# A Mixer and Expert Block on One Core: 32 Early Expert Chunks Instead of 24, Low Parts on VectorE, Small Groups Normed with the Dense Frames

## The chip, the cores and the metric

The kernel runs on one core of one Trainium2 chip. TensorE multiplies matrices, VectorE (DVE) and ScalarE (ACT) work on tiles, GpSimd (POOL) does some tile work and issues the indirect gathers, SyncE (SP) issues transfers. The metric is the device time of one execution in microseconds.

## The reference, cut to what matters

512 frames of width 2048 go through one layer (an RWKV mixer and a sparse attention, gated and projected) and then a PEER feed-forward with 16384 experts and a final RMSNorm. The change touches the feed-forward and the norm:

```
def _peer_ffn(h, w_query, sub_keys, expert_u, expert_v):
    q = (h @ w_query).reshape(B, T, PEER_HEADS, 2, PEER_HALF)      # 8 heads, 2 halves of 128
    s = einsum('bthcq,hcnq->bthcn', q, sub_keys)                   # 128 sub-keys per half
    s1, i1 = top_k(s[..., 0, :], 16); s2, i2 = top_k(s[..., 1, :], 16)
    cand = s1[..., :, None] + s2[..., None, :]
    top_s, pos = top_k(cand, 16); eid = i1*128 + i2 at pos
    gate = softmax(top_s)
    act = gelu(einsum('nd,nhkd->nhk', hx, expert_u[eid]), exact)
    return einsum('nhk,nhkd->nd', gate * act, expert_v[eid])

h = h + _peer_ffn(rmsnorm(h), ...)
return rmsnorm(h)
```

## The kernel before, in words

All large products take a float32 weight tile of 128 x 1024 apart into a high part (ScalarE, line 204) and a low part (VectorE, line 206; in the head loop GpSimd, line 208) and run three matmuls per pair of factors: high by high, high by low, low by high. `load_w` loads the tile on SyncE's queue and raises the priority of its three instructions by 100, which puts them that much ahead in the order of their engines. Each engine runs its instructions in a fixed order. `pieces` hands out a product of 2048 rows in four pieces of 12 matmuls.

The first 1700 us (mixer, attention, projection) are not touched. Then:

*Head loop* (`route`, lines 1122 to 1175). For each of 8 heads and 2 halves: the sub-keys are loaded (line 1128), the query is computed (48 matmuls of 512 columns), then the scores, and on VectorE the 16 best by `top16`. From the two halves the 16 best pairs follow (lines 1141 to 1168). After each head four pieces of the early chunks and two items (below) are put in.

*Early chunks* (`early`, list EARLY). An expert chunk e is 128 experts; `act` multiplies its 2048 x 128 keys with the 336 dense frames and applies gelu. A group `cg` has 8 chunks, 16 groups in all. For 24 chunks this is done already in the route, and the activations are saved to memory (d_a): the first two of each even group, the first of each odd one.

*Gate phase* (lines 1201 to 1225). 84 turns of four frames each: ScalarE, GpSimd and VectorE make one-hot masks (`oa`, `ob`), TensorE multiplies them to gates (`pg`, eight instructions a turn), ScalarE copies them to Gs, and after every fourth turn they go to memory (d_g). 64 pieces of the early chunks are spread evenly over the 84 turns, and every sixth turn has one item.

*Pack* (lines 1006 to 1010). ScalarE and VectorE copy the frames of the dense part into ph and pl.

*Dense stage* (`experts`). 336 frames go through all experts. For each group the gates G are loaded (1253), the activations of the 8 chunks are computed (the early ones loaded from d_a, line 1271), multiplied with G and split (`gated`), and then for each of 16 blocks of 128 output columns 8 x 3 matmuls add up the values (1293 to 1295) and VectorE adds them to accT (1300). In the first group the early chunks stand last.

*Items* (`gathered`). The other 176 frames take their experts' rows one by one: GpSimd gathers 128 rows of 8 KB (line 1040, three buffers `rows`), VectorE multiplies and sums them (1050, `up`) or adds them to `out` (1062, `down`). They are three groups (GROUPS): 128 frames with all 128 rows, 32 frames in four parts, 16 frames in eight parts. The small groups are folded by TensorE (1074), added to the residual, normed and stored (1076 to 1083). `step` calls an item so often that all are through shortly before the end; an item's instructions stand behind the last low part.

*End* (`turned`, `final`). The dense result is transposed, the residual added, normed, and stored: two tiles of 128 frames and one of 80.

## Time and profile before

| | |
|---|---|
| median of 3 runs | 4027.23 us (4023.66 to 4030.58) |
| the profiled execution | 4027.87 us, span 4026.1 us |
| TensorE busy | 3873.1 us (96%), mean granted clock 0.987 |
| VectorE busy | 2851.7 us (71%) |
| ScalarE busy | 1399.9 us (35%) |
| GpSimd busy | 1076.6 us (27%) |
| transfers | 946.17 MB, mean 235 GB/s |

Busy times are sums over the whole span and say nothing of which engine limits a stage. Matmuls are pipelined and overlap in the records, so the pace of TensorE is read from how many start in a stretch. Lines as L1223 are lines of the kernel; `wk`, `mm` and `po` are the tiles in TensorE's accumulators (`po` belongs to the early chunks). A row of a timeline gives the start, the length, the engine (a q behind it: its queue), the line, the tiles and, in brackets, the engine's idle time before it and what ended that.

### The profile page before, as it was taken

How to read it: one execution, taken by the hardware profiler on the slowest of the kernel's cores; microseconds unless marked ns; L12 is line 12 of the kernel's file. 1: busy time of each engine (PE TensorE's matmuls, PEld its weight loads, DVE VectorE, ACT ScalarE, POOL GpSimd, SP SyncE). 2: the span in 40 equal slices, each digit the busy share in tenths (PEclk: the TensorE clock that was granted, in tenths of full speed). 3: DMA queues.
4: the chain of work that ended last, by engine and by line, in shares of the span. 5: the costliest groups of instructions: out<-in, count | busy, mean ns of one | idle time of the engine just before them, and what ended most of it. 6: DMA issues, size and time to landing. Idle time of an engine off the chain costs nothing.

```text
span 4026.1 us, 57532 instructions
## 1 busy us (share of the span) xinstructions
PE 3873.1 (96%) x22241; PEld 3505.8 (87%) x22241; DVE 2851.7 (71%) x4738; ACT 1399.9 (35%) x2048; POOL 1076.6 (27%) x1012
## 2 busy tenths in 40 slices
PE   7999999999999999999989799999999999999998
PEld 6787778888887788777879799999999999999998
DVE  5445589434444553379988689888788978998885
ACT  4222323222324422232278333333323333333333
POOL 2000211101004300064367233233233323333320
PEclk9999999999999999999999899999999999999999
DMA  4343852333226443374478799999999989999994
GB/s 149 119 134 123 196 181 81 96 107 95 90 83 211 140 138 139 105 260 162 169 220 269 277 350 371 369 369 366 323 342 366 371 302 358 372 366 367 368 346 153
DMA packets 258290, 946.17 MB, mean 235 GB/s; under 512 B 28224, under 2 KB 77504, under 8 KB 209280
## 3 DMA queue, kind: packets, MB, share of 16 engines
q1 hardware_dynamic: 132528, 445.76, 31.9%
q0 software_dynamic: 82144, 474.71, 31.8%
q10 hardware_dynamic: 43344, 22.02, 1.9%
q8 instruction: 175, 2.87, 0.3%
q14 instruction: 99, 0.81, 0.1%
HBM read 866.18 MB, written 76.12 MB: 234 GB/s over the span
## 4 chain that ended last, share of the span: by engine, by line
PE 39%; DMA 4%; DVE 3%; issue 2%; ACT 1%; POOL 1%; DVEq 0%; SPq 0%; ACTq 0%; POOLq 0%
PE wk L1293 7%; PE wk L1295 7%; PE wk L1294 7%; PE mm L224 5%; PE mm L225 5%; PE mm L223 5%; DMA rows<-in_rv_dram,eid 2%; PE wk L1223 1%; DMA rows<-in_ru_dram,eid 1%; POOL rows L1040 1%; DVE wlo L206 1%; DVE out L1062 1%; PE po L223 1%; PE po L224 1%; PE po L225 1%
## 5 line engine op out<-in xcount | busy, mean ns | idle before, releaser
L204 ACT ACTIVATE whi<-raw 128x1024 fp32r<-128x1024 f32 x758 | 803.2, 1061 | 1902.2 <-PE mm L224 1015.7
L206 DVE TENSOR_TENSOR wlo<-raw,whi 128x1024 fp32r<-128x1024 f32 x726 | 890.1, 1227 | 630.1 <-ACT whi L204 567.6
L1293 PE MATMUL wk<-Wh,whi 128*128 128x336 f32 x2048 | 653.9, 320 | 25.7 <-ACT Wh L236 25.7
L1294 PE MATMUL wk<-Wl,whi 128*128 128x336 f32 x2048 | 650.9, 318 | 4.7 <-DVE Wl L237 4.7
L1295 PE MATMUL wk<-Wh,wlo 128*128 128x336 f32 x2048 | 650.6, 318 | 0.2 <-DVE wlo L206 0.2
L223 PE MATMUL mm<-ph,whi 128*128 128x336 f32 x1664 | 526.7, 317 | 7.1 <-ACT ph L1009 7.1
L225 PE MATMUL mm<-ph,wlo 128*128 128x336 f32 x1664 | 527.3, 317 | 1.5 <-DVE wlo L206 1.5
L224 PE MATMUL mm<-pl,whi 128*128 128x336 f32 x1664 | 526.6, 316 | 0.0
L223 PE MATMUL mm<-xh,whi 128*128 128x512 f32 x1168 | 473.4, 406 | 2.8 <-ACT xh L355 1.5
L225 PE MATMUL mm<-xh,wlo 128*128 128x512 f32 x1168 | 468.5, 401 | 6.0 <-DVE wlo L206 6.0
L224 PE MATMUL mm<-xl,whi 128*128 128x512 f32 x1168 | 470.5, 403 | 0.6 <-POOL xl L357 0.5
L1040 POOL DMA_INDIRECT rows<-in_rv_dram,eid x176 | 284.0, 1613 | 593.0 <-DVE out L1062 494.7
L1062 DVE SCALAR_TENSOR_TENSOR out<-rows,act,out 128x2048 f32<-128x2048 f32 x173 | 406.0, 2347 | 41.6 <-DMA rows<-in_rv_dram,eid 40.8
L1040 POOL DMA_INDIRECT rows<-in_ru_dram,eid x176 | 273.2, 1552 | 602.9 <-DVE act L1050 486.4
L1050 DVE CUSTOM_DVE_ANT_0 rows<-rows,h2t 128x2048 f32<-128x2048 f32 x176 | 411.6, 2346 | 26.2 <-DMA rows<-in_ru_dram,eid 26.2
L1293 PEld LDWEIGHTS wk<-Wh,whi 128*128 128x128 f32 x2048 | 387.6, 190 | 29.4 <-ACT Wh L236 29.1
L1294 PEld LDWEIGHTS wk<-Wl,whi 128*128 128x128 f32 x2048 | 388.5, 190 | 6.7 <-DVE Wl L237 6.2
L1295 PEld LDWEIGHTS wk<-Wh,wlo 128*128 128x128 f32 x2048 | 388.6, 190 | 1.1 <-DVE wlo L206 0.7
L223 PEld LDWEIGHTS mm<-ph,whi 128*128 128x128 f32 x1664 | 313.3, 188 | 7.7 <-ACT ph L1009 7.3
L225 PEld LDWEIGHTS mm<-ph,wlo 128*128 128x128 f32 x1664 | 312.8, 188 | 1.9 <-DVE wlo L206 1.8
L224 PEld LDWEIGHTS mm<-pl,whi 128*128 128x128 f32 x1664 | 313.7, 189 | 0.5 <-issue 0.5
L225 PEld LDWEIGHTS mm<-xh,wlo 128*128 128x128 f32 x1168 | 221.8, 190 | 60.4 <-DVE wlo L206 6.9
(441 smaller groups left out, 6284.1 us busy)
## 6 DMA issues: line engine op xcount, KB each, us to landing
raw<-in_pu_dram SPq DMA_DIRECT2D x256, 512.0 KB
raw<-in_pv_dram SPq DMA_DIRECT2D x256, 512.0 KB
raw<-in_w_in_dram SPq DMA_DIRECT2D x146, 512.0 KB
d_g<-Gs ACTq DMA_DIRECT2D x21, 1024.0 KB
G<-d_g POOLq DMA_DIRECT2D x16, 1344.0 KB
raw<-in_wbr_dram SPq DMA_DIRECT2D x32, 512.0 KB
raw<-in_wout_dram SPq DMA_DIRECT2D x32, 512.0 KB
raw<-in_wpq_dram SPq DMA_DIRECT2D x32, 512.0 KB
```

Source lines behind the costliest of these rows:

```text
L204: nc.scalar.activation(hi, raw, AF.Copy)
L206: self.last = nc.vector.tensor_tensor(lo, raw, hi.bitcast(F32), op=ALU.subtract).ins
L223: nc.tensor.matmul(ps, hi[:, s], xh, start=k == 0, stop=False)
L224: nc.tensor.matmul(ps, hi[:, s], xl, start=False, stop=False)
L225: nc.tensor.matmul(ps, lo[:, s], xh, start=False, stop=k == nk - 1)
L1040: nc.gpsimd.indirect_dma_start(out=r, out_offset=None, in_=table, in_offset=bass.IndirectOffsetOnAxis(ap=eid[:, s:s + 1], axis=0))
L1050: v.tensor_tensor_reduce(r, r, h, 1.0, 0.0, op0=ALU.mult, op1=ALU.add, accum_out=self.act_[i][:, s:s + 1])
L1062: v.scalar_tensor_tensor(o, r, act[:, s:s + 1], o, op0=ALU.mult, op1=ALU.add)
L1223: mmul(pg[:, 128 * u:128 * u + 128], oa, ob, start=True, stop=True)
L1293: mmul(ps, hi[:, s], wh, start=j == 0, stop=False)
L1294: mmul(ps, hi[:, s], wl, start=False, stop=False)
L1295: mmul(ps, lo[:, s], wh, start=False, stop=j == 7)
```

## The change

EARLY has the first two chunks of every group, 32 in all. In the route 32 pieces lie in the head loop as before, 90 in the gate phase and 6 behind it. In the head loop the low parts of the query weights are made by VectorE as everywhere else, the sub-keys of all heads are loaded by one transfer ahead of it, and each head has one item instead of two; in the gate phase every seventh turn has an item instead of every sixth. In the first dense group the order of the chunks is 2 to 5, 0, 1, 6, 7, for the activations and for the value matmuls; the saved activations are loaded on ScalarE's queue. The two small groups no longer norm their frames: they store the sum with the residual to memory (d_s), it is loaded into the 48 free partitions of the last dense tile, and is normed and stored with it.

```diff
@@ -41,7 +41,7 @@
 
 GROUPS = ((160, 16, 8), (128, 32, 4), (0, 128, 1))
 
-EARLY = [8 * g + j for g in range(16) for j in range(2 - g % 2)]
+EARLY = [8 * g + j for g in range(16) for j in range(2)]
 
 VEC = {}
 _o = 0
@@ -169,7 +169,7 @@
     def __init__(self, tc, io, out, dbg=None):
         self.tc, self.nc, self.io, self.out, self.dbg = tc, tc.nc, io, out, dbg or {}
         self.fins = ExitStack()
-        self.wx, self.nw, self.low = None, 0, self.nc.vector
+        self.wx, self.nw = None, 0
         self.blocks = ((0, 128), (1, 128), (2, ND - 256))
 
     def pool(self, name, bufs=1, **kw):
@@ -202,10 +202,7 @@
             hi = ps.tile([128, 1024], F32R, tag="whi", name="whi")
             lo = ps.tile([128, 1024], F32R, tag="wlo", name="wlo")
             nc.scalar.activation(hi, raw, AF.Copy)
-            if self.low is nc.vector or wp is not self.wp:
-                self.last = nc.vector.tensor_tensor(lo, raw, hi.bitcast(F32), op=ALU.subtract).ins
-            else:
-                self.low.tensor_tensor(lo, raw, hi.bitcast(F32), op=ALU.subtract)
+            self.last = nc.vector.tensor_tensor(lo, raw, hi.bitcast(F32), op=ALU.subtract).ins
         return hi, lo
 
     def gemm(self, *a, **k):
@@ -308,6 +305,7 @@
             self.d_gate = d("d_gate", [16, 128, 2, 512])
             self.d_h = d("d_h", [T, D])
             self.d_h2 = d("d_h2", [NG, D])
+            self.d_s = d("d_s", [NG - 128, D])
             self.d_g = d("d_g", [ND // 16, 16, 128, 128])
             self.d_a = d("d_a", [len(EARLY), 128, ND])
             self.right = ExitStack()
@@ -1063,9 +1061,8 @@
                 else:
                     v.tensor_scalar(o, r, act[:, s:s + 1], None, op0=ALU.mult)
                 yield
-            h, g = get(), get()
+            h = row("h")
             nc.gpsimd.dma_start(h[:m], self.d_h[t0:t0 + m])
-            nc.gpsimd.dma_start(g[:m], io["gfin"].to_broadcast([m, D]))
             yield
             if parts > 1:
                 for q in range(4):
@@ -1073,14 +1070,17 @@
                     ps = self.wk()
                     nc.tensor.matmul(ps, self.fold[:, 128 * i:128 * i + 128], o[:, f], start=True, stop=True)
                     v.tensor_tensor(h[:m, f], ps[:m], h[:m, f], op=ALU.add)
-            else:
-                v.tensor_tensor(h, o, h, op=ALU.add)
+                nc.gpsimd.dma_start(self.d_s[t0 - 128:t0 - 128 + m], h[:m])
+                return
+            g = get()
+            nc.gpsimd.dma_start(g, io["gfin"].to_broadcast([128, D]))
+            v.tensor_tensor(h, o, h, op=ALU.add)
             s = self.gk.tile([128, 1, 1], F32, name="ss0")
-            sc.activation(o[:m], h[:m], AF.Square, accum_out=s[:m, 0])
+            sc.activation(o, h, AF.Square, accum_out=s[:, 0])
             yield
             yield
-            v.scalar_tensor_tensor(h[:m], h[:m], self.inverse(self.gk, s[:m]), g[:m], op0=ALU.mult, op1=ALU.mult)
-            nc.sync.dma_start(self.out[t0:t0 + m], h[:m])
+            v.scalar_tensor_tensor(h, h, self.inverse(self.gk, s), g, op0=ALU.mult, op1=ALU.mult)
+            nc.sync.dma_start(self.out[t0:t0 + m], h)
             yield
 
 
@@ -1118,14 +1118,13 @@
             tp = es3.enter_context(self.pool("top", 2))
             ts = tp.tile([128, 4, 8, 16], F32, name="ts", bufs=1)
             sel = [tp.tile([128, 4, 8, 16], F32, name=f"sel{i}", bufs=1) for i in range(2)]
-            self.low = nc.gpsimd
+            sk = tp.tile([128, 16, 128], F32, name="sk", bufs=1)
+            nc.gpsimd.dma_start(sk, io["subk"])
             for h in range(8):
                 sv = tp.tile([128, 2, 4, 16], F32, name="sv")
                 si = tp.tile([128, 2, 4, 16], U32, name="si")
                 sf = tp.tile([128, 2, 4, 16], BF16, name="sf")
                 for c in range(2):
-                    sk = tp.tile([128, 128], F32, name="sk")
-                    nc.gpsimd.dma_start(sk, io["subk"][:, 2 * h + c])
                     ps = self.mm()
                     self.gemm(ps, io["wpq"][2 * h + c], xs)
                     q = tp.tile([128, T], F32, name="pq", bufs=1)
@@ -1133,7 +1132,7 @@
                     pt = self.wk()
                     for tb in range(4):
                         s = slice(128 * tb, 128 * tb + 128)
-                        mmul(pt[:, s], q[:, s], sk, start=True, stop=True)
+                        mmul(pt[:, s], q[:, s], sk[:, 2 * h + c], start=True, stop=True)
                     S = tp.tile([128, T], F32, name="S")
                     sc.activation(S, pt, AF.Copy)
                     for tb in range(4):
@@ -1171,9 +1170,7 @@
                 for e, b in ((self.eid[-1], 0), (eid1, 1)):
                     m = e.shape[0]
                     v.scalar_tensor_tensor(e[:, 16 * h:16 * h + 16], sel[0][:m, b, h], 128.0, sel[1][:m, b, h], op0=ALU.mult, op1=ALU.add)
-                for _ in range(2):
-                    self.item()
-            self.low = v
+                self.item()
 
             sh = [128, 32, 16]
             tv = ts.rearrange("p b h k -> p (b h) k")
@@ -1202,10 +1199,10 @@
             Gs = gp.tile([128, 128, 16], F32, name="Gs")
             for b in range(4):
                 i = 4 * tg + b
-                n = 4 * len(EARLY) - 32
+                n = 4 * len(EARLY) - 32 - 6
                 for _ in range((i + 1) * n // (ND // 4) - i * n // (ND // 4)):
                     next(early, None)
-                if i % 6 == 5:
+                if i % 7 == 6:
                     self.item()
                 pg = self.wk()
                 for u in range(4):
@@ -1245,7 +1242,7 @@
         dp = self.dp
         self.due = 0
 
-        self.rate = (sum(2 * (128 // g[2]) + 4 for g in GROUPS) - self.nitems) / (256 + 2 * (128 - len(EARLY)) - 20)
+        self.rate = (sum(2 * (128 // g[2]) + 1 for g in GROUPS) + 3 - self.nitems) / (256 + 2 * (128 - len(EARLY)) - 20)
         ng = ND // 16
         for cg in range(16):
             first, last = cg == 0, cg == 15
@@ -1263,21 +1260,21 @@
 
             js = list(range(8))
             if first:
-                js = [j for j in js if 8 * cg + j not in EARLY] + [j for j in js if 8 * cg + j in EARLY]
+                js = js[2:6] + js[0:2] + js[6:8]
             for j in js:
                 e = 8 * cg + j
                 if e in EARLY:
                     a = self.gel.tile([128, ND], F32, tag="gel", name="gel")
-                    nc.sync.dma_start(a, self.d_a[EARLY.index(e)])
+                    nc.scalar.dma_start(a, self.d_a[EARLY.index(e)])
                 else:
                     a = run(self.act(e, self.mm()))
                 wait.append((j, a))
-                while len(wait) > (2 if first else 0):
+                while len(wait) > (2 if first and j in js[:6] else 0):
                     gated(*wait.pop(0))
                 if e not in EARLY:
                     self.step(2)
-            for w in wait:
-                gated(*w)
+            while wait:
+                gated(*wait.pop(0))
             turn = iter(())
             if last:
                 for _ in self.items:
@@ -1287,12 +1284,12 @@
             for db in range(16):
                 ps = self.wk()[:, 0:ND]
                 hi, lo = self.load_w(io["pv"][cg, db])
-                for j in range(8):
+                for j in js:
                     wh, wl = W[j]
                     s = slice(128 * j, 128 * j + 128)
-                    mmul(ps, hi[:, s], wh, start=j == 0, stop=False)
+                    mmul(ps, hi[:, s], wh, start=j == js[0], stop=False)
                     mmul(ps, hi[:, s], wl, start=False, stop=False)
-                    mmul(ps, lo[:, s], wh, start=False, stop=j == 7)
+                    mmul(ps, lo[:, s], wh, start=False, stop=j == js[-1])
                 a = self.accT[:, db]
                 if first:
                     sc.activation(a, ps, AF.Copy)
@@ -1312,9 +1309,10 @@
         self.gf = self.fp.tile([128, D], F32, name="gf")
         self.res = self.fp.tile([128, 3, D], F32, name="res")
         self.ssq = self.fp.tile([128, 3, 4], F32, name="ssq2")
-        nc.gpsimd.memset(self.ssq, 1.0)
         for tb, m in self.blocks:
             nc.gpsimd.dma_start(self.res[:m, tb], self.d_h[NG + 128 * tb:NG + 128 * tb + m])
+
+        nc.gpsimd.dma_start(self.res[ND - 256:, 2], self.d_s)
         nc.gpsimd.dma_start(self.gf, io["gfin"].to_broadcast([128, D]))
         yield
         for db in range(16):
@@ -1330,22 +1328,23 @@
             if db % 4 == 3:
                 q = db // 4
                 f = slice(512 * q, 512 * q + 512)
-                for tb, m in self.blocks:
-                    x = self.res[:m, tb, f]
-                    sc.activation(self.fp.tile([128, 512], BF16, name="sqf", bufs=2)[:m], x, AF.Square, accum_out=self.ssq[:m, tb, q:q + 1])
-                    v.tensor_tensor(x, x, self.gf[:m, f], op=ALU.mult)
+                for tb in range(3):
+                    x = self.res[:, tb, f]
+                    sc.activation(self.fp.tile([128, 512], BF16, name="sqf", bufs=2), x, AF.Square, accum_out=self.ssq[:, tb, q:q + 1])
+                    v.tensor_tensor(x, x, self.gf[:, f], op=ALU.mult)
             yield
 
     def final(self):
         nc = self.nc
         r = self.inverse(self.fp, self.ssq)
         for tb, m in self.blocks:
-            x = self.res[:m, tb]
+            x = self.res[:, tb]
             if tb == 1:
-                nc.scalar.activation(x, x, AF.Copy, scale=r[:m, tb:tb + 1])
+                nc.scalar.activation(x, x, AF.Copy, scale=r[:, tb:tb + 1])
             else:
-                nc.vector.tensor_scalar(x, x, r[:m, tb:tb + 1], None, op0=ALU.mult)
-            nc.sync.dma_start(self.out[NG + 128 * tb:NG + 128 * tb + m], x)
+                nc.vector.tensor_scalar(x, x, r[:, tb:tb + 1], None, op0=ALU.mult)
+            nc.sync.dma_start(self.out[NG + 128 * tb:NG + 128 * tb + m], x[:m])
+        nc.scalar.dma_start(self.out[128:NG], self.res[ND - 256:, 2])
         self.fins.close()
 
 
```

## Rows read from the trace of the kernel before

**Rows 1.** The page: busy time by engine, and GB/s in 40 slices of the span.
```profile
PE 3873.1 (96%) x22241; PEld 3505.8 (87%) x22241; DVE 2851.7 (71%) x4738; ACT 1399.9 (35%) x2048; POOL 1076.6 (27%) x1012
...
GB/s 149 119 134 123 196 181 81 96 107 95 90 83 211 140 138 139 105 260 162 169 220 269 277 350 371 369 369 366 323 342 366 371 302 358 372 366 367 368 346 153
```

**Rows 2.** Windows: length, PE, PEld, DVE, ACT, POOL busy (instructions), granted clock, DMA, GB/s.
```profile
1709.70:1984.40 274.70, 256.96 (x1275) 217.91 (x1274) 246.93 (x878) 78.18 (x99) 142.79 (x89) 0.98 0.59 202
...
1917.00:1949.80 32.80, 31.79 (x162) 27.05 (x161) 32.70 (x122) 8.87 (x11) 15.98 (x9) 1.00 0.49 170
...
1984.40:2024.60 40.20, 32.13 (x195) 30.54 (x195) 36.34 (x122) 15.19 (x24) 11.59 (x19) 0.96 0.51 171
...
2024.60:2232.30 207.70, 182.64 (x1303) 175.42 (x1301) 173.25 (x469) 156.59 (x288) 142.15 (x179) 0.98 0.77 243
...
2292.60:3905.00 1612.40, 1594.57 (x10229) 1584.37 (x10230) 1399.25 (x1363) 542.64 (x655) 512.72 (x333) 0.99 0.93 356
```

**Rows 3.** Timeline of TensorE, end of the gate phase: start, length, instruction, idle before.
```profile
2221.46 1.05 PE L1223 MATMUL wk<-ob,oa 128*128 128x128 f32 x8
...
2222.27 0.40 PE L223 MATMUL po<-h2h,whi 128*128 128x336 f32 x1
...
2224.19 1.05 PE L1223 MATMUL wk<-ob,oa 128*128 128x128 f32 x8
...
2232.32 0.65 PE L223 MATMUL mm<-ph,whi 128*128 128x336 f32 x1 [7.07 <-ACT ph L1009]
```

**Rows 4.** Windows of the early pieces alone, gate phase; no instruction on VectorE.
```profile
2024.60:2232.30 207.70, 111.95 (x631) 97.11 (x629) 0.00 (x0) 6.41 (x14) 0.98 0.77 243
```

**Rows 5.** Windows in the dense stage, columns as in the second group.
```profile
2295.40:2300.00 4.60, 4.60 (x16) 4.60 (x17) 0.51 (x1) 0.04 (x1) 1.28 (x1) 0.50 0.51 143
...
2400.00:2500.00 100.00, 100.00 (x649) 99.76 (x649) 89.36 (x98) 33.76 (x40) 30.30 (x21) 1.00 0.96 376
...
2900.00:2980.00 80.00, 73.77 (x448) 70.85 (x447) 58.42 (x76) 26.36 (x35) 23.75 (x13) 0.96 0.77 283
...
3250.00:3320.00 70.00, 65.73 (x394) 63.25 (x393) 52.84 (x62) 23.40 (x31) 21.80 (x12) 0.95 0.79 290
```

**Rows 6.** Timeline of the first expert group: SyncE, VectorE, TensorE.
```profile
2257.75 21.89 SPq L201 DMA_DIRECT2D raw<-in_pv_dram  x7
...
2279.69 0.95 SPq L1271 DMA_DIRECT2D gel<-d_a  x2
...
2291.49 0.51 DVE L1258 TENSOR_TENSOR gel<-gel,G 128x336 f32<-128x336 f32 x1 [5.39 <-DMA gel<-d_a]
...
2292.57 0.65 PE L1293 MATMUL wk<-Wh,whi 128*128 128x336 f32 x1 [14.30 <-ACT Wh L236]
...
2295.40 0.65 PE L1294 MATMUL wk<-Wl,whi 128*128 128x336 f32 x1 [2.18 <-DVE Wl L237]
```

**Rows 7.** Timeline of one head: VectorE, and GpSimd's subtraction.
```profile
1933.01 4.31 DVE L1050 CUSTOM_DVE_ANT_0 rows<-rows,h2t 128x2048 f32<-128x2048 f32 x1
...
1937.51 2.27 DVE L1050 CUSTOM_DVE_ANT_0 rows<-rows,h2t 128x2048 f32<-128x2048 f32 x1
...
1942.17 2.67 DVE L1162 CAST pf<-u 128x64 f32<-128x64 uint32 x1
...
1942.39 2.39 POOL L208 TENSOR_TENSOR wlo<-raw,whi 128x1024 fp32r<-128x1024 f32 x1
```

**Rows 8.** By line: duration in ns min/median/max, first and last start (the second 1849:1983).
```profile
L1162 DVE CAST pf<-u x8: 185/2646/2679, 1764.2 to 2007.9; 128x64 f32<-128x64 uint32 x8
...
L206 DVE TENSOR_TENSOR wlo<-raw,whi x8: 1206/1216/1220, 1860.3 to 1964.4; 128x1024 fp32r<-128x1024 f32 x8
```

**Rows 9.** Waits: us in total, times, longest (head loop, then dense stage).
```profile
PE mm L225 <- POOL wlo L208: 12.7, 6, 6.9
...
PE wk L1136 <- DMA sk<-in_subk_dram: 5.0, 1, 5.0
...
DVE out L1062 <- DMA rows<-in_rv_dram,eid: 40.8, 24, 5.4
```

## The prediction

> **What bounds the kernel now.** I read the page first. TensorE is busy for 96% of the span, and from the 24th of 40 slices to the last but one the transfers run at 302 to 372 GB/s [rows 1]. A share over the span decides nothing here, because the stages have different limits, so next I cut the span into the stretches that the change touches [rows 2] and asked of each what TensorE does.
>
> *Head loop* (1709.7 to 1984.4). One steady head takes 32.8 us; in it VectorE is busy for 32.70 and TensorE for 31.79 [rows 2]. VectorE is the bound, TensorE 3% behind.
>
> *Gate phase* (2024.6 to 2232.3, 207.7 us). In the order on TensorE a block of eight small matmuls takes 0.81 us (2221.46 to 2222.27) and the early piece behind it 1.92 us (2222.27 to 2224.19), back to back [rows 3]. 631 early matmuls lie in this stretch, 52.6 pieces of 12 [rows 4]. TensorE's work is thus 84 × 0.81 + 52.6 × 1.92 = 68.0 + 101.0 = 169.0 us; 38.7 us are idle. 7.07 of these are one gap at the end, before the first dense matmul [rows 3].
>
> *Dense stage* (2232.3 to 4008.5, 1776.2 us). Where nothing disturbs it, 649 matmuls start in 100 us: 154.1 ns each, at VectorE 89% and 376 GB/s [rows 5]. The stage's matmuls, 104 experts × 48 and 16 groups × 16 × 24, 11136 in all, are 1716 us at that pace. So it is bound by TensorE with 60 us lost, in three places: the first expert group (TensorE idle for 14.30 and 2.18 us [rows 6], and after that idle time 16 matmuls in 4.60 us at a granted clock of 0.50, 1.2 of 2.4 GHz [rows 5]: some 2.1 us lost; 18.6 together); the two ends of the small token groups (448 matmuls in 80 us and 394 in 70: 11 and 9 us [rows 5]); the rest scattered.
>
> **The change part by part.**
>
> *Eight more experts early.* The dense stage loses 8 × 48 = 384 matmuls: 384 × 0.1541 = **-59.2 us**. Beside them go 16 loads, and 16 high and 16 low parts; these were hidden.
>
> The same 384 matmuls, 32 pieces, come into the gate phase: 26 in its 84 turns, 6 behind it. Its TensorE work becomes 68.0 + 84.6 × 1.92 = 230.4 us. How much idle time stays? Bounds: none (230.4, +22.7; with the some 8 us that TensorE stands idle between 1984.4 and 2024.6 filled too, +15), or all 38.7 (+61.4). I take 8, since where a turn has a piece TensorE already runs without a gap, there is now a piece in every turn (90 in 84), and the six at the end lie over the 7.07 us gap. 230.4 + 8 - 207.7 = **+31**. The feeders allow it: VectorE is busy 173 of 207.7 us, ScalarE 157 [rows 2]; VectorE gets 13 × 1.22 and loses 2 items.
>
> *Low parts on VectorE, sub-keys at once, one item per head instead of two.* Per head VectorE gets four subtractions of 1.216 us [rows 8] (+4.9) and loses an item (2.3). While GpSimd does its 2.4 us subtraction, VectorE's instructions stretch: the cast takes 2.67 us beside it [rows 7] and 0.185 in the heads where it is alone [rows 8], the first item 4.31 and the second 2.27 [rows 7]. That goes: -2.5 and -2.0. Net -1.9 per head, VectorE at 30.8, and TensorE (31.79) is the next bound: at most 1.0 us a head. Against it: TensorE now waits for low parts that lie in VectorE's fixed order, behind candidate searches and a row that waits for its gather; what it waited for GpSimd is 12.7 us in all [rows 9]. Bounds: -13 (those waits gone), +21 (stretching stays: 8 × (4.9 - 2.3)). The one transfer of sub-keys is 1 MB where TensorE waited 5.0 us for the first 64 KB [rows 9]; at the loop's 202 GB/s [rows 2] a megabyte takes 5.2 us, so 0 to +5, taken as +2. Its queue (GpSimd's) loses 16 issues. I take -5 and +2: **-3**.
>
> *First expert group.* The saved activations now go out on ScalarE's queue and stand in the middle of the order; the value matmuls start with the chunks that are ready first. Before, the first waited on SyncE behind seven value loads whose buffers weren't free (2257.75, 21.89 us), went out at 2279.69 and was used at 2291.49, 11.8 us later [rows 6]. Now two whole experts (2 × 48 × 0.154 = 14.8 us of TensorE) follow their issue before the value matmuls need them. Of the 18.6 us I take **-17** (0 if the issue on ScalarE stalls as long). On ScalarE each issue waits for its tile's last reader; behind it wait only high parts, with the three buffers of high parts ahead.
>
> *Small groups normed with the dense frames.* Two norms go, each with a multiply over 2048 columns (about an item's 2.3 us), a dozen instructions on single columns and a square. More important, residual and gain no longer hold two of the three row buffers, so the next gathers need not wait for the norm. New: a store of the sum to memory, and the next group's rows need the buffer of `out`, free after the fold. GpSimd's store waits for four additions, with the next gathers queued behind it. Bounds -20 (both losses gone) and +10 (one as long again); I take **-6**. At the end one more transfer of 384 KB beside 2.6 MB in the tail: **+1** (0 to +3; at the 202 GB/s of the head loop 384 KB are 1.9 us).
>
> *More pressure in the dense stage.* Ten items move here: from 30 to 20 in the route, and the rate goes from 334/444 = 0.752 to 338/428 = 0.790 per weight load. One step of 24 matmuls (3.70 us) carries 0.790 × 2.3 = 1.82 us of row work instead of 1.73: VectorE goes from 89% to about 91.5%. Transfers: 356 GB/s × 1612.4 us [rows 2] = 574 MB; less 16 loads (-8.4), more 10 gathers (+10.5), more saved activations (+1.4): 577.5 MB in 1547 us is 373 GB/s. VectorE waits for late rows 40.8 us already [rows 9]. Below nothing only if fewer conflicts came of a faster stage, for which no row speaks. Bounds 0 and +40 (those waits doubled, all reaching TensorE); near the 100 us at 376 GB/s without a loss [rows 5], I take **+12**.
>
> **Sum.** -59 + 31 - 3 - 17 - 6 + 1 + 12 = -41. The profiled execution's span is 4026.1 us, its time 4027.87, within 0.7 of the median of the runs shown (4027.23). 4026.1 - 41 + 1.8 = 3987; I say **3986**.
>
> **The rivals.**
>
> *A. Transfers become the bound of the dense stage.* For: 373 GB/s over the whole stretch, group ends included, where two of 70 to 80 us run at 283 and 290 [rows 5]; outside these 383 are needed, and the page's best slice has 372 [rows 1]. Against: TensorE keeps 154 ns at 376. If 376 is the ceiling: (577.5 - 42.9) MB / 376 = 1422 us instead of 1397, +25 instead of +12: **about 4000**.
>
> *B. The gate phase can't take the pieces in.* Its turns are paced by the helpers' masks, so the new pieces add up whole: +61 instead of +31: **4016**. For: early in the phase TensorE does wait. Against: 2221 to 2224, where a piece and a block run without a gap [rows 3].
>
> *C. Slower: the saved activations come late in every group.* On ScalarE the issue stands behind the high parts of later chunks (`load_w` raises its instructions' priority by 100), so it goes out only when TensorE is in the next group; VectorE, in its fixed order, waits at the gating product, and the low parts behind it are late. Price: with the 11.8 us of [rows 6] and two chunks (7.4 us) in hand, 4.4 us in each of 15 groups: +66, **4052**. It decides from 41/15 = 2.7 us per group. Against: that landing stood behind 512 KB weight loads in its own queue.
>
> The Trainium skill (DMA: Bandwidth & Descriptors, "Issuing engines are not separate DMA queues") speaks for C: transfers of all issuers run on the same 16 engines, so another queue saves issue time only. By it the 11.8 us would stay and the sum would be C's. The trace of before can't show it, since no small load goes out on ScalarE in that stage.
>
> *D. A lower ceiling of the memory.* If the stage were held to the 356 GB/s that its long stretch shows [rows 2], 577.5 MB would take 1622 us, and the 59 and 6 us saved there would be lost: +31 - 3 - 17 + 1 + 10 = +22, **4050**. The 376 GB/s of 100 us in a row speak against it [rows 5].
>
> The Trainium skill (same page, "Where 436 GB/s comes from") puts a core's share of memory at about 358 GB/s, 435 being the fabric's; by the former D would hold. The trace disagrees, 376.
>
> **How the numbers follow.** Forecast 63% (3955 to 4003), A 17%, B 10%, C 7%, D 3%. The range 3955 to 4020 takes in A and B; C and D stay outside, and some of the low end, where the head loop and the group ends give all they can. This measurement can tell 0.2% (8 us) from no change, so faster ends at 4019: the forecast, most of A, half of B: 0.83; same 0.07 (the other half of B, the edge of A); slower 0.10 (C, D).
>
> **What would show it.** Right: the gate phase 230 to 245 us long and without the gap at its end; no PE idle time over 3 us in the first expert group; the cast at 0.19 us in every head; 10752 dense matmuls, still 154 ns. Wrong: a gate phase of 260 us or more (B); VectorE waiting for the saved activations in most groups (C); bins at 370 GB/s with TensorE above 160 ns (A, D); heads longer than 33 us (low parts too late on VectorE).

## The result: 0.8% faster, by other terms than forecast

The changed kernel takes 3994.12 us (median, 3985.83 to 4000.98; before 4025.84), a ratio of 0.9923 [0.9909, 0.9937]. The profiled execution took 3985.83 us with a span of 3984.1. The page:

```profile
PE 3857.8 (97%) x22241; PEld 3492.8 (88%) x22241; DVE 2843.3 (71%) x4742; ACT 1398.7 (35%) x2044; POOL 996.7 (25%) x965
...
GB/s 151 119 136 117 206 176 88 89 106 103 88 73 208 144 140 144 73 273 152 129 224 248 269 364 378 378 378 383 382 318 397 372 349 387 368 376 374 378 342 153
```

Windows of it, columns as in [rows 2]: head loop, one steady head, the passage to the gate phase, gate phase up to the first dense matmul, dense stage, tail.

```profile
1705.90:1959.20 253.30, 247.53 (x1266) 212.53 (x1267) 238.14 (x906) 79.95 (x101) 38.76 (x35) 1.00 0.56 191
1896.50:1928.00 31.50, 31.50 (x162) 27.25 (x161) 30.54 (x125) 8.88 (x11) 2.97 (x3) 1.00 0.41 140
1961.40:1995.40 34.00, 27.39 (x168) 26.18 (x167) 30.85 (x104) 14.27 (x22) 10.16 (x18) 0.95 0.41 132
1995.40:2250.70 255.30, 243.98 (x1715) 239.13 (x1713) 192.07 (x484) 181.11 (x312) 145.84 (x178) 0.99 0.74 236
2250.70:3963.00 1712.30, 1682.19 (x10810) 1666.51 (x10811) 1498.59 (x1493) 578.17 (x712) 557.10 (x359) 1.00 0.94 359
3963.00:3984.10 21.10, 1.17 (x8) 0.64 (x7) 8.09 (x23) 3.95 (x7) 0.00 (x0) 0.62 0.43 149
```

Measured between the same marks in the kernel before (where these differ from [rows 2], the marks stand in brackets): head loop 273.9 (1708.2 to 1982.1) to 253.3, passage 40.2 to 34.0, gate phase 207.7 to 255.3, dense stage 1775.4 (2232.3 to 4007.7) to 1712.3, tail 18.4 to 21.1. The steady head is now TensorE's (31.50 of 31.50).

TensorE's waits, first in the gate phase, then in the dense stage (us in total, times, longest):

```profile
PE po L220 <- ACT gel L1231: 6.2, 8, 1.4
PE wk L1220 <- ACT oa L1216: 3.6, 4, 1.9
...
PE wk L1292 <- DVE wlo L205: 13.3, 12, 3.0
PE wk L1290 <- ACT Wh L233: 10.8, 11, 2.1
PE wk L1291 <- DVE Wl L234: 4.2, 5, 1.4
PE mm L220 <- ACT ph L1007: 1.2, 1, 1.2
```

The 14.30 us of [rows 6] and the 7.07 us of [rows 3] are gone (1.2 is left). What replaces them is small and often: value matmuls (L1290 to L1292) start 28 times a little late, 28.3 us in all, nearly all of the 30.1 us that TensorE is not busy in the stage (1712.30 less 1682.19).

### The profile page after: what moved, and what is told of

Read it like the earlier page. It is cut to its first block, busy times and chain, and to the rows that moved or that the text cites. A ratio compares the mean times of both kernels' runs of the same rounds, so it can differ in the third digit from the quotient of the medians.

```text
span 3984.1 us, 57536 instructions
## 1 busy us (share of the span) xinstructions
PE 3857.8 (97%) x22241; PEld 3492.8 (88%) x22241; DVE 2843.3 (71%) x4742; ACT 1398.7 (35%) x2044; POOL 996.7 (25%) x965
## 4 chain that ended last, share of the span: by engine, by line
PE 57%; issue 17%; DMA 10%; POOL 7%; DVE 7%; ACT 2%; SPq 0%; POOLq 0%; DVEq 0%; ACTq 0%
PE mm L221 10%; PE mm L222 10%; PE mm L220 10%; POOL rows L1038 6%; DMA rows<-in_rv_dram,eid 5%; PE wk L1292 3%; PE wk L1291 3%; PE wk L1290 3%; PE po L220 2%; PE po L221 2%; PE po L222 2%; DVE wlo L205 2%; PE wk L1220 2%; PE wk L876 2%; PE wk L878 1%
## 5 line engine op out<-in xcount | busy, mean ns | idle before, releaser
L205 DVE TENSOR_TENSOR wlo<-raw,whi 128x1024 fp32r<-128x1024 f32 x758 | 927.2, 1224 | 597.5 <-ACT whi L204 525.7
L1292 PE MATMUL wk<-Wh,wlo 128*128 128x336 f32 x2048 | 652.1, 319 | 13.3 <-DVE wlo L205 13.3
L1290 PE MATMUL wk<-Wh,whi 128*128 128x336 f32 x2048 | 651.6, 319 | 10.8 <-ACT Wh L233 10.8
L222 PE MATMUL mm<-ph,wlo 128*128 128x336 f32 x1536 | 486.5, 317 | 1.8 <-DVE wlo L205 1.7
L220 PE MATMUL mm<-ph,whi 128*128 128x336 f32 x1536 | 484.9, 316 | 1.2 <-ACT ph L1007 1.2
L221 PE MATMUL mm<-pl,whi 128*128 128x336 f32 x1536 | 485.6, 316 | 0.0
L1048 DVE CUSTOM_DVE_ANT_0 rows<-rows,h2t 128x2048 f32<-128x2048 f32 x176 | 401.3, 2285 | 46.5 <-DMA rows<-in_ru_dram,eid 46.0
L1292 PEld LDWEIGHTS wk<-Wh,wlo 128*128 128x128 f32 x2048 | 387.1, 189 | 18.3 <-DVE wlo L205 17.1
L1290 PEld LDWEIGHTS wk<-Wh,whi 128*128 128x128 f32 x2048 | 386.2, 189 | 14.9 <-ACT Wh L233 14.2
L222 PEld LDWEIGHTS mm<-ph,wlo 128*128 128x128 f32 x1536 | 288.3, 188 | 2.7 <-DVE wlo L205 2.6
L220 PEld LDWEIGHTS mm<-ph,whi 128*128 128x128 f32 x1536 | 288.7, 188 | 1.8 <-ACT ph L1007 1.8
L221 PEld LDWEIGHTS mm<-pl,whi 128*128 128x128 f32 x1536 | 289.1, 188 | 0.0
```

Source lines behind the costliest of these rows:

```text
L205: self.last = nc.vector.tensor_tensor(lo, raw, hi.bitcast(F32), op=ALU.subtract).ins
L220: nc.tensor.matmul(ps, hi[:, s], xh, start=k == 0, stop=False)
L221: nc.tensor.matmul(ps, hi[:, s], xl, start=False, stop=False)
L222: nc.tensor.matmul(ps, lo[:, s], xh, start=False, stop=k == nk - 1)
L1048: v.tensor_tensor_reduce(r, r, h, 1.0, 0.0, op0=ALU.mult, op1=ALU.add, accum_out=self.act_[i][:, s:s + 1])
L1290: mmul(ps, hi[:, s], wh, start=j == js[0], stop=False)
```

## The experiments

The **excess** of a dense stage is its length less its matmuls at the 0.1541 us of [rows 5]: 11136 with 24 early chunks (1716.1 us), 10752 with 32 (1656.9). Gate phase as in the windows above, up to the first matmul on the packed frames (ph); times in us. Medians are of different batches; in each the kernel before ran too, and its median stands beside. The interval of a ratio to it reaches some 6 us to either side, so smaller differences between two rows are not shown. The last three columns are of one profiled execution each.

| kernel | median | before, beside it | gate phase | dense | excess |
|---|---|---|---|---|---|
| before | 4025.84 | | 207.7 | 1775.4 | 59 |
| changed, as profiled above | 3994.12 | 4025.84 | 255.3 | 1712.3 | 55 |
| changed, again | 3991.43 | 4024.19 | 255.2 | 1721.7 | 65 |
| 24 chunks | 3980.43 | 4024.19 | 208.3 | 1749.6 | 34 |
| low parts on GpSimd | 4002.70 | 4024.19 | 255.2 | 1716.2 | 59 |
| first group as before | 3992.73 | 4024.19 | 255.4 | 1722.1 | 65 |
| two items per head | 3992.21 | 4026.50 | 254.0 | 1712.1 | 55 |
| 24, two accumulators | 3984.94 | 4026.50 | 211.3 | 1755.2 | 39 |
| half the gathers | 3944.07 | 4026.50 | 255.0 | 1670.4 | 14 |
| short row operations | 3989.32 | 4026.50 | 255.1 | 1718.1 | 61 |
| 24, small groups as before | 3991.24 | 4024.55 | 208.7 | 1758.6 | 43 |
| 24, more gate items | 3996.70 | 4024.55 | 219.8 | 1760.0 | 44 |
| 32, more gate items | 3982.52 | 4024.55 | 258.3 | 1708.3 | 51 |
| 24, G through ScalarE | 3987.11 | 4025.55 | 207.7 | 1756.8 | 41 |

**The changed kernel again.** 

> The changed kernel once more, unaltered. Theory: its three stages have fixed lengths: query heads (first to last query matmul) 253, gate phase (first to last gate matmul) 255, dense part (first pu to last pv matmul) 1712 us, each within 4 us, and a median between 3984 and 4001. Rival: the profile that was read is of a lucky execution and the other executions lose their 10 us in one stage, which then stands longer here by 8 us or more.

3991.43 (3988.92 to 3996.09). The gate phase repeats within 0.1 us and the sub-key matmuls span 233.8 instead of 231.2; the dense stage was 1712.3 and is 1721.7, as the rival had it:

```profile
2251.50:3973.20 1721.70, 1688.59 (x10809) 1674.33 (x10810) 1499.61 (x1493) 577.84 (x712) 562.03 (x359) 0.99 0.93 357
```

So the stage that varies from execution to execution is the dense one, and where two kernels' excesses lie less than 10 us apart, only the medians speak. TensorE's clock goes with it: the granted clock is 1.00 above and 0.99 here. Inside the stage it stood at 0.50, the lower of its two levels, for 10.2 us in all above and for 30.7 us here, each time after TensorE had waited for operands. Twenty microseconds more at half the pace are worth up to 10 us, most of the 9.4 us between the two.

**24 chunks.**
```diff
-EARLY = [8 * g + j for g in range(16) for j in range(2)]
+EARLY = [8 * g + j for g in range(16) for j in range(2 - g % 2)]
```


> The change with the 24 early chunks of before; all other parts stay. Theory (a chunk's TensorE work only moves: 8 x 48 matmuls x 0.1541 us = 59 us leave the dense part, and come back in the gate phase with 32 pieces whose price is what the gate phase grew by, 48 us): gate phase back to about 208, dense part +59 to 1771, query heads still 253, time +11 against the changed kernel (some 4005). Rival (the early chunks make the whole gain, and the gate phase takes them nearly for nothing): gate phase stays near 240, time +32 or more (4026).

3980.43 (3978.67 to 3985.69), a ratio of 0.9894 [0.9879, 0.9909] to before; the changed kernel beside it 0.9917 [0.9904, 0.9931], 3988.92 at the least. Both expectations missed. Gate phase, dense stage:

```profile
1999.30:2207.60 208.30, 186.70 (x1302) 178.90 (x1302) 171.62 (x469) 157.09 (x291) 132.73 (x178) 0.98 0.75 231
2207.60:3957.20 1749.60, 1735.47 (x11193) 1723.79 (x11194) 1520.09 (x1509) 598.95 (x736) 556.86 (x359) 1.00 0.93 355
```

The gate phase gives back the 47 us, as the theory had it; the dense stage, with 59 us more of matmuls, is only 28 to 37 longer. The eight extra chunks cost 11 us (no run with 24 chunks is as slow as the fastest of the changed kernel).

**Low parts on GpSimd, one item per head.**
```diff
-            self.last = nc.vector.tensor_tensor(lo, raw, hi.bitcast(F32), op=ALU.subtract).ins
+            if self.low is nc.vector or wp is not self.wp:
+                self.last = nc.vector.tensor_tensor(lo, raw, hi.bitcast(F32), op=ALU.subtract).ins
+            else:
+                self.low.tensor_tensor(lo, raw, hi.bitcast(F32), op=ALU.subtract)
...
+            self.low = nc.gpsimd
             for h in range(8):
```


> The change with the low parts of the query weights on GpSimd again, still one gather item per head and the sub-keys loaded at once. VectorE's sum per head: 30.5 less four subtractions of 1.21, plus the two stretches seen before (a row operation of 2.27 that took 4.31, a cast of 0.19 that took 2.67) = 30.2 us, under TensorE's 31.4. Theory (a head is the longer of TensorE's and VectorE's sum, and what made it 32.8 was the second item): query heads stay at 253 to 258, time +0 to +5. Rival (the stretching beside GpSimd or PE's waits for the low parts set the head): heads of 32.8 again, query heads 265 or more, time +12 or more.

4002.70 (3997.53 to 4004.61), +11, but not in the heads, which take 31.5 us each after the first, as the theory had it; both forecasts of the time missed. One head, and an instruction of VectorE that still stretches beside GpSimd's subtraction (3.16 us in most heads, 0.22 at the least); then TensorE's wait and GpSimd's issue of the sub-keys:

```profile
1889.50:1921.00 31.50, 31.50 (x162) 27.15 (x161) 31.30 (x119) 8.91 (x12) 11.16 (x6) 1.00 0.41 141
L1161 DVE SCALAR_TENSOR_TENSOR pf<-u,u x8: 218/3162/3174, 1761.5 to 1984.2; 128x64 f32<-128x64 uint32 x8
```
```profile
PE wk L1139 <- DMA sk<-in_subk_dram: 5.7, 1, 5.7
```
```profile
1722.41 0.54 POOL L1125 DMA_DIRECT2D sk<-in_subk_dram  x1
```

In the changed kernel run again that issue is at 1717.67 and TensorE waits 1.9:

```profile
1717.67 0.53 POOL L1122 DMA_DIRECT2D sk<-in_subk_dram  x1 [1.95 <-ACT whi L204]
```

So with the low parts on GpSimd, this issue goes out 4.7 us later: the first sub-key matmul is 5.8 us later (1735.2, 1729.4), the passage to the gate phase 3.7 longer. The profiled execution was the fastest of five; the rest of the 11 us is not located.

**The first group as before.**
```diff
-                js = js[2:6] + js[0:2] + js[6:8]
+                js = js[2:8] + js[0:2]
...
-                    nc.scalar.dma_start(a, self.d_a[EARLY.index(e)])
+                    (nc.sync if first else nc.scalar).dma_start(a, self.d_a[EARLY.index(e)])
...
-                for j in js:
+                for j in range(8):
```


> The change with the first expert group as before: its chunks in the old order (the two saved ones last, all held back by two), its value matmuls from chunk 0 on, and its two saved activations loaded through SyncE. Theory (the 17 us that TensorE stood in the first group of the kernel before, 14.30 + 2.18 of them, come from there alone): the idle stretch at the start of the first value matmuls returns, dense part +12 to +17, time +12 to +17. Rival (the wait ends elsewhere, since the gate matrix and the packed activations are ready earlier now): +0 to +5.

3992.73, +1.3: the rival's number, though the idle stretch is back in its place. TensorE, and SyncE's issue:

```profile
2306.38 0.65 PE L1290 MATMUL wk<-Wh,whi 128*128 128x336 f32 x1 [13.13 <-ACT Wh L233]
```
```profile
2294.83 0.92 SPq L1268 DMA_DIRECT2D gel<-d_a  x2
```

The first group loses 17.8 us here and 11.7 in the changed kernel run again (in its value matmuls instead), the other fifteen groups 47.5 and 53.1. Whether the stall really lets the gathers catch up, or the two executions merely differ, isn't settled.

**Two items per head.**
```diff
-                self.item()
+                for _ in range(2):
+                    self.item()
```


> The change with two gather items per head again (low parts on VectorE, 32 chunks). VectorE's sum per head then is 30.5 + 2.3 for the second row operation = 32.8 us against TensorE's 31.4. Theory (a head takes the longer of the two sums; the item alone made the head loop of before long): the undisturbed heads go from 31.3 to 32.7, query heads +9 to +12 us; eight items fewer are left for the dense part, which gives back 0 to 5; time +4 to +12. Rival (the item costs nothing where the low parts are on VectorE, because nothing is stretched beside GpSimd): heads stay at 31.3, time -5 to 0.

3992.21 (3981.97 to 3998.18), +0.8: the heads as the theory had them, the time nearer to the rival's. A head, the loop, the dense stage:

```profile
1837.00:1870.00 33.00, 31.74 (x164) 27.26 (x163) 33.00 (x125) 9.06 (x12) 5.15 (x3) 1.00 0.48 166
1705.00:1972.60 267.60, 256.20 (x1287) 219.31 (x1287) 254.66 (x923) 81.32 (x103) 55.16 (x43) 0.98 0.60 212
2261.70:3973.80 1712.10, 1682.59 (x10810) 1666.45 (x10811) 1482.21 (x1477) 578.48 (x712) 547.40 (x351) 1.00 0.92 354
```

VectorE fills the heads again, and the sub-key matmuls span 241.9 us instead of 233.8: the second item made the heads long. The time is the same, with a dense stage at the low end of what it does without the edit: consistent with eight gathers fewer there, not shown by one execution.

**Two accumulators, 24 chunks.**
```diff
-self.pso.tile([128, 512], F32, tag="po", name="po")
+self.pso.tile([128, 512], F32, tag="po", name="po") if i < 8 else self.mm()
```


> 24 early chunks, and from the ninth chunk on the early chunks take turns on two accumulators instead of one. In the run with 24 chunks TensorE waited 8.3 us (7 times) in the gate phase for the gelu that frees the one accumulator. Theory: these waits go, gate phase 194 to 186 to 189, time 3980 to 3972 to 3976. Rival (the blocks' operands, which ScalarE and GpSimd make, are late in their place: 9.4 us of waits for oa are there already): gate phase within 3 of 194, time unchanged.

3984.94, 4.5 slower than with one accumulator, but 2.2 when each is taken against the kernel before beside it; the ratios are 0.9895 [0.988, 0.991] and 0.9894 [0.9879, 0.9909], so no difference is shown. TensorE's waits in the gate phase (9.6 us for the gelu with one accumulator), then the first dense matmul, gate phase and dense stage:

```profile
PE wk L1220 <- ACT oa L1216: 11.2, 17, 1.7
PE wk L1220 <- POOL oa L1213: 6.1, 11, 1.1
PE wk L1220 <- DVE oa L1218: 2.2, 3, 1.5
...
2207.16 0.42 PE L220 MATMUL mm<-ph,whi 128*128 128x336 f32 x1 [4.06 <-ACT ph L1007]
...
1995.90:2207.20 211.30, 186.12 (x1299) 175.10 (x1297) 170.54 (x466) 155.17 (x292) 129.93 (x178) 0.99 0.73 229
2207.20:3962.40 1755.20, 1738.76 (x11193) 1727.09 (x11194) 1520.68 (x1509) 599.26 (x736) 556.25 (x359) 1.00 0.92 354
```

The gelu is gone from the list, and the masks, 11.3 us before, are 19.5. With another accumulator free more pieces lie among the turns; only 20 matmuls are left behind the last of them to cover the packing, and TensorE waits 4.06 us for it (1.2 with one accumulator). The phase is 3.0 us longer, the dense stage 5.6, which is less than it varies by. The theory missed: the waits moved to the next operand and the gain with them. The rival has the time right, but not the phase: from the first gate matmul to the last it lasts 204 us, not 194.

**Half the gathers; short row operations** (32 chunks; `short` is set in the dense stage, and `down` has the same edit).
```diff
+            if self.short and self.nitems % 2:
+                return self.held
-            r = get()
+            r = self.held = get()
```
```diff
+                w = slice(0, 512 if self.short else D)
-                v.tensor_tensor_reduce(r, r, h, 1.0, 0.0, op0=ALU.mult, op1=ALU.add, accum_out=self.act_[i][:, s:s + 1])
+                v.tensor_tensor_reduce(r[:, w], r[:, w], h[:, w], 1.0, 0.0, op0=ALU.mult, op1=ALU.add, accum_out=self.act_[i][:, s:s + 1])
```


> 32 chunks, and in the dense part every second gathered row block is not fetched: the row operation runs on the block fetched before it (wrong sums for the 208 gathered frames). VectorE's work is the same (1498 us of the dense 1712), the gathers' bytes there are halved (about 334 blocks of 1 MB become 167; 359 GB/s on average become some 265). The dense part stands 55 to 65 us over its matmuls at 0.1541 us with 32 chunks, 33 with 24. Theory (the transfers are at their limit: rows land late, VectorE stands on them, low parts and gated weights come late): the excess falls to 25 or less, dense part 1682 or less. Rival (VectorE's own work is too much for the shorter groups): excess 50 or more, dense part 1705 or more.

> 32 chunks, all rows fetched, but in the dense part the row operations work on 512 of the 2048 columns (wrong sums for the gathered frames): VectorE is relieved of some 334 x 2.27 x 3/4 = 570 us of its 1498. Theory (transfers at their limit): the excess of the dense part stays at 45 or more, dense part 1702 or more, and the row operations' waits for rows grow. Rival (VectorE's work): excess 25 or less, dense part 1682 or less. If both this and the kernel with half the gathers fall, it takes both: late rows, and a VectorE without room to catch up.

Half the gathers: 3944.07 (two runs), the dense stage, then the time from a gather's issue to its landing (min, median, max):

```profile
2251.20:3921.60 1670.40, 1669.07 (x10809) 1662.10 (x10810) 1502.87 (x1493) 580.39 (x712) 308.47 (x194) 1.00 0.73 264
```
```profile
DMA to landing us min/median/max: 5.2/7.8/10.8
```

The same of the changed kernel, with all of them:

```profile
DMA to landing us min/median/max: 5.3/9.6/18.5
```

VectorE's waits for rows there; with half the gathers the list has none:

```profile
DVE out L1060 <- DMA rows<-in_rv_dram,eid: 46.1, 22, 5.6
DVE rows L1048 <- DMA rows<-in_ru_dram,eid: 41.0, 24, 6.3
```

Short row operations: 3989.32 (two runs), dense stage, TensorE's largest wait, and VectorE's for rows:

```profile
2252.50:3970.60 1718.10, 1685.87 (x10810) 1672.37 (x10811) 1013.47 (x1493) 579.47 (x712) 390.38 (x359) 0.99 0.93 358
```
```profile
PE wk L1294 <- DVE wlo L205: 25.2, 14, 3.5
...
DVE out L1062 <- DMA rows<-in_rv_dram,eid: 52.4, 38, 3.6
DVE rows L1049 <- DMA rows<-in_ru_dram,eid: 42.6, 33, 2.6
```

VectorE's 485 us less change nothing; the gathers' halving takes nearly the whole excess, at the same VectorE work (1503). Both theories hold: the dense stage loses its time to late transfers. Whether it is the bytes or the order in GpSimd's queue that makes them late, this pair can't tell, since half the gathers are also half the issues (GpSimd busy for 308.47 us instead of 557.10).

**The small groups as before, 24 chunks.** The edit takes back what the diff does in `gathered`, `turned` and `final`, and to the rate; its core:
```diff
-                nc.gpsimd.dma_start(self.d_s[t0 - 128:t0 - 128 + m], h[:m])
-                return
...
+            sc.activation(o[:m], h[:m], AF.Square, accum_out=s[:m, 0])
...
+            nc.sync.dma_start(self.out[t0:t0 + m], h[:m])
```


> 24 early chunks, and the two small groups of gathered frames normed and written by themselves as before (the rest as changed). Between the kernel before and the one with 24 chunks, TensorE's loss around the ends of the small groups (sixth, seventh and tenth expert group) went from 28 to 10 us, and the tail after the last value matmul grew from 18.4 to 21.1. Theory (these ends are where VectorE stood in chains of short steps): dense part +8 to +14, tail -2.5, time +6 to +11 (3986 to 3991). Rival (the dense part is as long as its bytes take at some 357 GB/s, wherever it stalls): dense part within 4 of 1750, time -3 to +2.

3991.24 (3988.55 to 3995.05), +10.8 (10.4 against the kernel before beside each): the theory. The dense stage is 9.0 longer, the tail 2.7 shorter. Dense stage and tail:

```profile
2209.90:3968.50 1758.60, 1738.32 (x11193) 1726.28 (x11194) 1527.95 (x1537) 603.82 (x740) 560.71 (x359) 1.00 0.92 354
3968.50:3986.90 18.40, 1.24 (x9) 0.70 (x7) 8.08 (x23) 3.95 (x7) 0.00 (x0) 0.66 0.39 150
```

**More items in the gate phase.**
```diff
-                if i % 7 == 6:
+                if i % 4 == 3:
```
(with 32 chunks: `i % 3 == 2`)


> 24 early chunks, and 21 gather items in the gate phase instead of 12: nine row blocks of 1.05 MB are fetched before the dense part. Theory (the dense part takes its bytes at 355 to 359 GB/s: 621 MB in 1750 us, and 1.05 MB are 2.9 us, down to its 1716 us of matmuls): dense part -15 to -26; VectorE has 26 us free in the 194 us of the gate phase and nine row operations take 21, gate phase 0 to +8; time 3958 to 3975. Rival (the gate phase has no room: late one-hot operands stand on row operations whose rows are late): gate phase +15 or more, time 3978 or more.

> 32 early chunks, and 28 gather items in the gate phase instead of 12: sixteen row blocks fewer in the dense part. Theory (as for the kernel with 24): 614 MB less 16.8 are 597, at 357 GB/s 1673 us against 1657 us of matmuls, dense part -30 to -45 (1675 to 1690); the gate phase is bound by TensorE (241 us, of which VectorE works 188) and takes 16 row operations of 2.3 us with 0 to +8; time 3953 to 3970, so the 32 chunks are worth it once the gathers make room. Rival (the dense part's loss with 32 chunks is in its shorter groups, not in its bytes): dense part -10 or less, time 3982 or more.

With 24: 3996.70, with 32: 3982.52 (3975.47 to 3990.34). Gate phase and dense stage of each:

```profile
1996.80:2216.60 219.80, 195.44 (x1318) 187.00 (x1316) 192.57 (x478) 159.07 (x294) 157.56 (x187) 0.94 0.83 266
2216.60:3976.60 1760.00, 1739.17 (x11193) 1727.16 (x11194) 1503.10 (x1491) 599.11 (x736) 530.89 (x350) 1.00 0.91 348
```
```profile
2000.90:2259.20 258.30, 240.81 (x1693) 235.71 (x1691) 227.61 (x514) 178.67 (x315) 185.34 (x194) 0.99 0.88 292
2259.20:3967.50 1708.30, 1684.84 (x10810) 1672.59 (x10811) 1465.89 (x1461) 579.65 (x712) 518.82 (x343) 0.99 0.92 350
```

The theory of a fixed byte rate falls: with 24 chunks the stage moved less, at 348 GB/s instead of 355, and took 10 us longer. 14.7 us of its loss are in the seventh group, where a small group of frames ends; GpSimd, with the next gathers behind it, waits there for the fold (in the run with 24 chunks and 12 items that group loses 4.3, and the same wait is 3.27):

```profile
2897.68 0.56 POOL L1045 DMA_DIRECT2D h2t<-d_h  x1 [14.71 <-PE wk L1071]
```

So where the gathers stand may count, not only their bytes. The gate phase grew by 11.5 us with 24 chunks and by 3 with 32. Most of the 11.5 goes with TensorE's clock: granted 0.94 in the phase against 0.98 with 12 items, and 0.04 of 220 us are some 8. With 32 chunks the dense stage is 4 to 13 us shorter where 30 to 45 were forecast, the rival's numbers. The version with 32 chunks is 9 us faster than the changed kernel, with some runs of the two overlapping, and level with 24 chunks alone (ratios 0.9891 [0.9876, 0.9906] and 0.9894).

**G through ScalarE, 24 chunks.** The reason for it lies in the run with 24 chunks: GpSimd's issues, and VectorE.

```profile
2372.57 1.46 POOL L1250 DMA_DIRECT2D G<-d_g  x1
2374.66 1.00 POOL L1038 DMA_INDIRECT rows<-in_ru_dram,eid  x1 [0.63 <-DVE act L1048]
```
```profile
2392.51 2.29 DVE L1048 CUSTOM_DVE_ANT_0 rows<-rows,h2t 128x2048 f32<-128x2048 f32 x1 [5.63 <-DMA rows<-in_ru_dram,eid]
```
```diff
-            nc.gpsimd.dma_start(G.rearrange("p g e t -> p g (e t)"), self.d_g[:, cg].rearrange("g p f -> p g f"))
+            nc.scalar.dma_start(G.rearrange("p g e t -> p g (e t)"), self.d_g[:, cg].rearrange("g p f -> p g f"))
```


> 24 early chunks, and each group's gate matrix G (1.34 MB) loaded through ScalarE's queue instead of GpSimd's, where the row gathers run in order behind it. In the run with 24 chunks a gather issued 2.1 us behind such a load (2374.66) held VectorE until 2392.51, 5.6 us of idling, and three groups in a row show the same 5 to 6 us. Theory (the losses at the starts of the value matmuls come from gathers queued behind G): VectorE's waits for rows fall from 74 us to 50 or less, the dense part's excess from 33 to 20 or less, time 3965 to 3972. Rival (the bytes set it; G takes its share of the engines from either queue, and ScalarE's own order gains one more wait): waits and excess unchanged, time 3976 to 3986.

3987.11, 6.7 slower, 5.3 against the kernel before beside each; the ratios' intervals overlap (0.9898 [0.9882, 0.9915]), so that it is slower is not shown, but the forecast gain is not there. VectorE's waits in the dense stage, G's and the gathers' times to landing (24 chunks on GpSimd: 74.4 us for rows; the changed kernel: G 15.2 us, gathers up to 18.5), and VectorE's one long wait:

```profile
DVE rows L1048 <- DMA rows<-in_ru_dram,eid: 23.5, 21, 3.3
DVE gel L1255 <- DMA G<-d_g: 19.2, 3, 12.2
DVE out L1060 <- DMA rows<-in_rv_dram,eid: 15.6, 18, 3.5
```
```profile
G<-d_g ACTq DMA_DIRECT2D x15, 0.5 KB, 25.3
```
```profile
DMA to landing us min/median/max: 5.9/9.6/14.2
```
```profile
2831.30 0.51 DVE L1255 TENSOR_TENSOR gel<-gel,G 128x336 f32<-128x336 f32 x1 [12.19 <-DMA G<-d_g]
```

The waits for rows halve, to 39 us, and groups two to five lose nothing (0.4 us; 2.3 before the edit); then one G, issued at 2803.78, is there only at 2831.30, and TensorE loses 9 us in the sixth group. Half the theory holds: the order within GpSimd's queue makes rows late. But TensorE had little to gain by it, and in this execution lost more to the late G.

## Why the prediction was right

The number was right (3994, forecast 3986, range 3955 to 4020) because errors cancelled, which is luck: the chunks were to bring 16 us (-59 + 31 + 12) and cost 11; the other parts were to bring 25 (-3 - 17 - 6 + 1) and, with 24 chunks, brought 44 (4024.19 beside that run, to 3980.43). Undone one at a time (the small groups with 24 chunks, the others with 32), these give back 11 (low parts), 11 (small groups), 1 (first group) and 1 (second item). Some 20 of the 44 us are thus put down to no part: the sub-keys in one transfer, the saved activations on ScalarE's queue and the items' spacing were not undone by themselves, nor the low parts and the second item together.

- *Dense matmuls, -59, and pressure, +12.* The pace held, 59.2 us of matmuls went. Pressure was mis-sized: between 24 and 32 chunks the stage fell by 28 to 37, so 22 to 31 came back, inside the bounds 0 to +40 and at their far end. The experiments that halve the gathers and that shorten VectorE's work put the excess of the stage with 32 chunks on late transfers. That is close to rival A, which gave 4000; but A's ceiling of 376 GB/s isn't one, with a slice at 397. Of the eleven slices of the page that move 370 GB/s or more there, nine hold 155 to 157 ns per matmul; two, at 372 and 387, show the sign named for A, 164 to 165.
- *Gate phase, +31; measured 47.6.* The step that was wrong is the idle time to be filled. The prediction read 38.7 us of it from the price of one turn (0.81 and 1.92); the row that it quotes has TensorE busy for 182.64 of 207.70 us [rows 2], which leaves 25.1. Now it is busy for 243.98 of 255.30, which leaves 11.3, not far from the 8 forecast. So 14 us were filled where the prediction filled 31, and at its own prices the phase would hold 68.0 + 86.9 × 1.92 = 234.9 us of work (1715 matmuls less 672 are 86.9 pieces, 2.3 more than assumed) and 20.4 of the rest. Of the 11.3 idle, 9.8 are in the waits above: the single accumulator, which the prediction overlooked, and the masks; freeing the first, with 24 chunks, only lengthened the second. 255 lies above the 230 to 245 named as the sign of being right, and rival B (+61) was about as far off on the other side.
- *Head loop, -3; measured -20.6.* What was forecast of the engines came: the cast takes 0.19 us in every head, VectorE is at 30.54 (30.8 forecast), TensorE is next. Size wrong twice: "at most 1.0 us a head" became 1.4, and eight steady heads were taken for the loop, in which one head took 41.0 us and now takes 31.3. But the low parts are not what shortened the heads: with one item they are as short with the low parts on GpSimd, stretching included (31.5), and with two items they are long without it (33.0). The credit is the item's. The passage, 6.2 shorter, had no term in the sum. The cast row:

```profile
L1161 DVE CAST pf<-u x8: 185/187/189, 1755.8 to 1979.2; 128x64 f32<-128x64 uint32 x8
```

- *First group, -17.* The stall went, but undoing this part changes the time by 1.3, less than the noise: removing a stall was booked as its length.
- *Small groups, -6; tail, +1.* Undone together, the time grows by 10.8; the tail alone was lengthened by 2.7 (18.4 to 21.1), so the groups brought 9.0 (the dense stages of two executions) to 13.5 (the medians), more than forecast.
- *Rivals C and D.* VectorE waited for a saved activation once in the dense stage, 1.3 us; C is out. For D the stage's average is 354 to 359 GB/s in most runs, and yet a stage with fewer bytes ran longer at 348: not a ceiling that sets the time. The Trainium skill (DMA: Bandwidth & Descriptors, "Where 436 GB/s comes from") has about 358; as an average the runs agree with it, as a limit at each moment the slice of 397 does not.

The lowest median of a kernel that does all the work is that of the change with its first line taken back: 24 chunks, 3980.43 us, 1.1% under the kernel before; 32 chunks with more gate items can't be told from it.

## What to carry to other kernels

Work moved from one stage to another that the same engine bounds gains only the receiver's idle time, which a stage without it shows; read that time from the engine's busy sum, not from the price of one turn; ask also whether the giver, with less to do, meets a second limit. Price a stall by undoing it, not by its length, where another resource is nearly full; and sum the loop that is there, not its steady turn times its count. A right total proves no term.

## What the hardware showed beyond that

- A gather of 1 MB lands 9.6 us after issue (median) while the 16 engines are 94% busy, 7.8 at 73%.
- Rows issued 2.1 us behind a 1.34 MB load on the same queue landed 17.8 us after issue. On ScalarE's queue that load took 25.3 us instead of 15.2, and the gathers' longest time was 14.2 (24 chunks) where it is 18.5 in the changed kernel (32). The Trainium skill (DMA: Bandwidth & Descriptors, "Issuing engines are not separate DMA queues") says that the transfers of all issuers run on the same 16 engines and that another issuer saves only the time of starting them; the stage's average agrees, 354 GB/s with the load on ScalarE's queue and 355 without, while VectorE's waits for rows, 39 us instead of 74, show that the order within a queue is worth something.
- A slice of the changed kernel (99.6 us) moved 397 GB/s, on one core; with the short row operations the same slice moved 407.
- Waits cost TensorE twice: it stands, and its granted clock then falls, for 10.2 and 30.7 us at 0.50 in the dense stages of the two executions of the changed kernel. With half the gathers it is 1.00 throughout the stage.
